# Strassen products on two halves of tokens, large down blocks and interleaved attentions in a one-core decoder step

## The chip, the cores and the metric

The kernel runs on one core of one Trainium2 chip. The metric is the device time of one execution in microseconds; less is better. The profile shows TensorE (PE, with its weight loads as PEld), VectorE (DVE), ScalarE (ACT), GpSimd (POOL), SyncE (SP) and the DMA engines. SBUF is the memory on the chip, PSUM holds what TensorE adds up.

## The reference

One layer of a hybrid decoder over 1104 tokens: 1040 of a prompt and 8 x 8 sample tokens, whose keys and values lie in a paged cache of 1024 positions for each of 8 sequences. All is float32, the model width 1024, the hidden width 2816.

```python
def layer(x, ...):
    x = x + 0.5 * rmsnorm(swiglu(rmsnorm(x, f1_pre), f1_wg, f1_wu, f1_wd), f1_post)
    m = mixer(rmsnorm(x, m_pre), w_in, ...)
    x = x + rmsnorm(m, m_post)
    x = x + 0.5 * rmsnorm(swiglu(rmsnorm(x, f2_pre), f2_wg, f2_wu, f2_wd), f2_post)

def swiglu(x, w_gate, w_up, w_down):
    return (jax.nn.silu(x @ w_gate) * (x @ w_up)) @ w_down

def mixer(h, ...):
    q, k, v, gate_b, gate_c, hc = jnp.split(h @ w_in, ...)      # 3072 columns
    o = rmsnorm(attend(q, k, v, lam), subln_g) * (1.0 - lambda_init)
    u_ext = concatenate([conv_prev, gate_c * hc], axis=1)
    y = sum(conv_w[j] * u_ext[:, j:j + t] for j in range(3))
    return concatenate([o, gate_b * y], axis=-1) @ w_out
```

`attend` is differential attention with 4 heads: for each head two softmax maps with 64 features of keys each, a weighted difference of the two, times 128 features of values. The prompt attends to itself causally, each sample sequence to its cached pages and its own new tokens.

## The kernel before, in words

Activations are kept with features on the partitions, in 8 chunks of 128, and tokens along the free dimension, in three groups `TG` of 376, 424 and 304. The array multiplies float32r, so every operand is kept as a high and a low half, and `three` (L187) makes a product of three matmuls, on lines 188, 189 and 190. `split_unit` (L170) loads 512 KB of weights, copies the high half (ACT, L177) and subtracts for the low one (POOL or DVE, L178).

A feed-forward (`ffn`, L343) goes through 11 blocks of two 128-wide hidden units. For each unit and group, `products` (L312) makes the gate and the up products, 24 matmuls into one PSUM bank; `gate` (L354) multiplies by 1 / rms, applies Silu, and multiplies again on POOL; `up_now` (L376) multiplies and splits the hidden values (DVE L381, ACT L382, DVE L383). `down` (L385) adds up two hidden units for each of 8 output chunks and 3 groups and adds the sum to `ys` in SBUF (DVE, L394). The hidden values never leave SBUF.

Between two phases stands `junction` (L258), for each token group: a mean over features by a matmul, a normalisation with the residual (DVE L279, POOL L280), high and low halves of the next phase's input (ACT, DVE L256), and sums of squares (L229). `meet` (L322) and the strings `FIRST`, `MEET1`, `MEET2`, `LAST` and `FINAL` (L70 to L76) write out by hand in which order the products of the last block, the junctions of the three groups and the first units of the next phase stand; `in_turn` ties a product behind the one before it on TensorE. Else a scheduler orders each engine's instructions.

The mixer makes q, k and v (12 units), stores high and low halves of q and k in DRAM, then makes the convolution's 12 units; the stages of the sample's attention stand between them (`turns`, L893): scores, weights, values and a gather for each of four pairs of sequences, with cache pages of 256 KB loaded ahead. Then comes the prompt's attention, 36 steps of head and query tile (`prompt_jobs`, L657): scores with high and low halves stacked on 128 rows (L675, L676), mask and maximum (DVE L684), exponents (ACT L696), difference of maps (POOL L700, DVE L701), transposes (L713), products with the values (L728). Between these steps stand the output projection's products for the convolution half (`conv_part`, L937). The rest of the output projection (`out_proj`, L1003) leads into the second feed-forward.

## Time and profile before

| | us |
|---|---|
| median of 3 runs | 2295.68 |
| lowest and highest of them | 2293.51, 2296.21 |
| span of the profiled execution | 2293.3 |
| PE busy in it | 2200.7 |
| DVE busy | 1064.4 |
| ACT busy | 601.9 |
| POOL busy | 656.0 |

The span is the time from the first to the last instruction of the one execution that was profiled; it lies 2.4 us under the median of the runs. A busy time is the sum over an engine's instructions with overlaps counted once. Matmuls are pipelined: the duration in a row is longer than the distance to the next start, so the pace of TensorE is read from starts.

### The profile page before, as it was taken

Reading aid. Unit: us, or ns where it says so; the run is one execution under the profiler, and the core shown is the slowest. Engines: PE = TensorE matmul, PEld = TensorE weight load, DVE = VectorE, ACT = ScalarE, POOL = GpSimd, SP = SyncE. Lnnn points to the kernel's source line nnn. Section 1 sums busy time; section 2 is a strip of 40 time slices with the busy share of each in tenths; the row PEclk is TensorE's granted clock in tenths of the full one; section 3 lists DMA queues with packets and bytes.
Section 4 is the critical chain, followed back from the end, with each engine's and each line's share of the span. In section 5 each row is a group of like instructions: output and inputs, shape, how many; then the busy total and the mean of one; then the engine's idle time right before and its main releaser. Section 6 shows DMA issues by size and latency. Waiting matters only on the chain.

```text
span 2293.3 us, 33252 instructions
## 1 busy us (share of the span) xinstructions
PE 2200.7 (96%) x13542; PEld 2126.0 (93%) x13542; DVE 1064.4 (46%) x1900; ACT 601.9 (26%) x1116; POOL 656.0 (29%) x487
## 2 busy tenths in 40 slices
PE   8999999999999899998998999899999999999995
PEld 7999999999999888997777899799999999999995
DVE  7333444343443587122226687943344343433347
ACT  6411111111111344211115565542111111111122
POOL 6222211222122355322223215641211222122215
PEclk9999999999999999998998999899999999999998
DMA  5101111111101142656677624421111111101113
GB/s 179 56 28 56 47 46 31 44 55 47 47 28 47 51 135 93 241 171 213 200 214 182 175 93 154 143 71 46 47 47 39 36 56 46 47 28 46 56 37 131
DMA packets 85387, 201.24 MB, mean 88 GB/s; under 512 B 18546, under 2 KB 38258, under 8 KB 82674
## 3 DMA queue, kind: packets, MB, share of 16 engines
q1 hardware_dynamic: 85234, 199.12, 27.3%
q8 instruction: 106, 1.74, 0.3%
q14 instruction: 47, 0.39, 0.1%
HBM read 161.80 MB, written 37.29 MB: 87 GB/s over the span
## 4 chain that ended last, share of the span: by engine, by line
PE 83%; DVE 8%; DMA 4%; ACT 2%; issue 1%; SPq 1%; POOL 1%; DVEq 0%; POOLq 0%; ACTq 0%
PE mm L188 18%; PE mm L189 18%; PE mm L190 18%; PE dn L188 8%; PE dn L189 8%; PE dn L190 8%; DVE y L279 3%; PE po L728 1%; DVE al L256 1%; DVE ss L229 1%; DMA raw<-oc_spill 1%; PE fl L713 1%; DMA raw<-in_w_out 1%; DMA qk<-qk_spill 1%; PE qk L675 1%
## 5 line engine op out<-in xcount | busy, mean ns | idle before, releaser
L189 PE MATMUL mm<-al,w 128*128 128x376 f32 (+2 forms) x2640 | 878.8, 333 | 16.1 <-DVE al L256 16.0
L188 PE MATMUL mm<-ah,w 128*128 128x376 f32 (+2 forms) x2640 | 880.4, 334 | 7.8 <-ACT w L177 5.4
L190 PE MATMUL mm<-ah,w 128*128 128x376 f32 (+2 forms) x2640 | 875.4, 332 | 0.5 <-DVE w L178 0.5
L189 PEld LDWEIGHTS mm<-al,w 128*128 128x128 f32 x2640 | 499.2, 189 | 29.2 <-DVE al L256 23.3
L188 PEld LDWEIGHTS mm<-ah,w 128*128 128x128 f32 x2640 | 499.1, 189 | 23.2 <-issue 8.7
L190 PEld LDWEIGHTS mm<-ah,w 128*128 128x128 f32 x2640 | 499.4, 189 | 6.7 <-DVE w L178 1.3
L178 POOL TENSOR_TENSOR w<-raw,w 128x1024 fp32r<-128x1024 f32 (+1 forms) x118 | 278.0, 2357 | 701.5 <-ACT w L177 696.9
L394 DVE TENSOR_TENSOR y<-y,dn 128x376 f32<-128x376 f32 (+2 forms) x480 | 255.3, 536 | 315.9 <-PE dn L190 315.5
L189 PE MATMUL dn<-w,w 128*128 128x376 f32 (+2 forms) x1056 | 350.1, 332 | 7.9 <-DVE w L383 7.9
L188 PE MATMUL dn<-w,w 128*128 128x376 f32 (+2 forms) x1056 | 348.6, 331 | 3.9 <-DVE y L394 3.9
L190 PE MATMUL dn<-w,w 128*128 128x376 f32 (+2 forms) x1056 | 349.7, 332 | 0.0
L177 ACT ACTIVATE w<-raw 128x1024 fp32r<-128x1024 f32 (+1 forms) x166 | 168.0, 1026 | 507.3 <-PE mm L189 224.7
L362 POOL TENSOR_TENSOR w<-w,R 128x376 f32<-128x376 f32 (+1 forms) x132 | 131.2, 996 | 582.4 <-ACT w L361 525.5
L361 ACT ACTIVATE w<-w 128x376 f32<-128x376 f32 (+1 forms) x132 | 66.0, 506 | 571.5 <-DVE w L357 571.4
L189 PEld LDWEIGHTS dn<-w,w 128*128 128x128 f32 x1056 | 199.4, 189 | 10.6 <-DVE w L383 8.6
L188 PEld LDWEIGHTS dn<-w,w 128*128 128x128 f32 x1056 | 199.1, 189 | 7.2 <-DVE y L394 5.1
L190 PEld LDWEIGHTS dn<-w,w 128*128 128x128 f32 x1056 | 199.4, 189 | 1.9
L357 DVE TENSOR_TENSOR w<-mm,R 128x376 f32<-128x376 f32 (+1 forms) x132 | 70.9, 540 | 260.1 <-PE mm L190 259.9
L383 DVE TENSOR_TENSOR w<-w,w 128x376 fp32r<-128x376 f32 (+1 forms) x132 | 148.7, 1129 | 66.8 <-ACT w L382 66.7
L381 DVE TENSOR_TENSOR w<-w,mm 128x376 f32<-128x376 f32 (+2 forms) x126 | 67.6, 536 | 225.1 <-PE mm L190 224.4
L382 ACT ACTIVATE w<-w 128x376 fp32r<-128x376 f32 (+2 forms) x132 | 66.5, 505 | 239.2 <-DVE w L381 239.2
L280 POOL TENSOR_TENSOR y<-y,xr 128x376 f32<-128x376 f32 (+2 forms) x66 | 81.8, 1269 | 47.4 <-DVE y L279 47.4
(153 smaller groups left out, 1875.2 us busy)
## 6 DMA issues: line engine op xcount, KB each, us to landing
raw<-in_w_gu SPq DMA_DIRECT2D x86, 512.0 KB, 3.7
raw<-in_w_dn SPq DMA_DIRECT2D x44, 512.0 KB, 3.6
kp<-in_cache_k SPq DMA_DIRECT2D x64, 256.0 KB, 4.5
vp<-in_cache_v SPq DMA_DIRECT2D x64, 256.0 KB, 4.7
raw<-in_w_in SPq DMA_DIRECT2D x24, 512.0 KB, 5.7
qk<-qk_spill SPq DMA_DIRECT2D x38, 260.0 KB, 6.2
qk_spill<-hl SPq DMA_DIRECT2D x8, 1040.0 KB, 4.1
w<-qk_spill SPq DMA_DIRECT2D x10, 260.0 KB, 7.9
```

What stands on the lines that cost most here:

```text
L177: nc.scalar.activation(hi[:, s], raw[:, s], AF.Copy)
L178: low_on.tensor_tensor(lo[:, s], raw[:, s], hi[:, s].bitcast(F32), op=ALU.subtract)
L188: nc.tensor.matmul(ps, lh, rh, start=first, stop=False)
L189: nc.tensor.matmul(ps, lh, rl, start=False, stop=False)
L190: last_pe[0] = nc.tensor.matmul(ps, ll, rh, start=False, stop=last).ins
L279: nc.vector.scalar_tensor_tensor(x, x, gains[:, g_post, c:c + 1], r, op0=ALU.mult, op1=ALU.mult)
L280: (nc.gpsimd if g_pre is not None or c < 6 else nc.vector).tensor_tensor(x, x, xs[c], op=ALU.add)
L357: nc.vector.tensor_tensor(g, pg, a[i][2], op=ALU.mult)
L362: nc.gpsimd.tensor_tensor(g, g, r, op=ALU.mult)
L381: nc.vector.tensor_tensor(v, v, pu, op=ALU.mult)
L383: nc.vector.tensor_tensor(hl, v, hh.bitcast(F32), op=ALU.subtract)
L394: nc.vector.tensor_tensor(ys[i][:, d, :], ys[i][:, d, :], ps, op=ALU.add)
```

## The change

The tokens are now two halves of 552, each of two quarters of 276 (`G`). The gate and the up product of a hidden unit, or two units of the input projection (`PAIRS`), are made for one half of tokens as a 2 x 2 block product by a Strassen scheme (Winograd's form): the input features in two halves, the two units, the two quarters of tokens. There are seven products instead of eight, each over 4 chunks of features and 276 tokens. Some are added up in a shared PSUM bank (`STEPS`), the others are combined on ACT and DVE (`Parts`, with `Hidden` for feed-forwards and `Unit2`, `Product`, `Gated` for the mixer). Both operands need sums: `weights_piece` adds quarters of the weights on DVE and splits each of the seven operands (ACT copy, DVE subtract, both 512 wide) into the only weight set there is, piece n behind product n of the unit before; `quarters_of` does the same once for each phase with the activations of a half.

```diff
+    STEPS = [("a", J_P1), ("b", J_Q5), ("a", J_Q6), ("c", J_P2), ("a", J_Q7), ("b", J_P3), ("a", J_Q4)]
+
+    def product(ps, p, j, first):
+        x14 = lay["x14"][p]
+        for k in range(4):
+            s = slice(k * P, (k + 1) * P)
+            three(ps, wset[:, j, 0, s], wset[:, j, 1, s], x14[:, 7 + j, k, :], x14[:, j, k, :],
+                  first and k == 0, k == 3, skip_group_check=True)
+
...
+        for i, (u, p) in enumerate(jobs):
+            change = i + 1 < len(jobs) and jobs[i + 1][0] != u
+            if p:
+                for _ in background:
+                    pass
+            use = uses(u, p)
+            banks = {}
+
+            def step(n, p=p, use=use, banks=banks):
+                tag, j = STEPS[n]
+                first = tag not in banks
+                if first:
+                    banks[tag] = bank("mm")[:, :G]
+                in_turn(product, banks[tag], p, j, first)
+                use(n, banks[tag])
+
+            def last(step=step, change=change):
+                step(6)
+                if change:
+                    weights_piece(6)
+                    order.pop(0)
+                    if order:
+                        weights_of(src(order[0]))
+
+            for n in range(6):
+                step(n)
+                if n == 0 and pending:
+                    pending()
+                if change:
+                    weights_piece(n)
+                for _ in range(BG):
+                    next(background, None)
+            pending = last
+        pending()
+        for _ in background:
+            pass
```

```diff
+    def weights_piece(n):
+
+        a11, a12, a22, a21 = [wraw[:, q, :] for q in range(4)]
+        a3 = WR[:, 2048:2560]
+        if n == 0:
+            dve.tensor_tensor(a3, a11, a21, op=ALU.add)
+        elif n == 1:
+            dve.tensor_tensor(a21, a21, a22, op=ALU.add)
+        elif n == 2:
+            dve.tensor_tensor(a11, a11, a21, op=ALU.add)
+        elif n == 5:
+            dve.tensor_tensor(a12, a12, a11, op=ALU.add)
+        halves(wset[:, n, 0, :], wset[:, n, 1, :], (a11, a21, a11, a12, a3, a12, a22)[n], dve)
...
+        def split(j, raw):
+            halves(x14[:, 7 + j, ks, :], x14[:, j, ks, :], raw, dve)
+
+        dve.tensor_tensor(t[0], b11, b12, op=ALU.subtract)
+        dve.scalar_tensor_tensor(t[1], t[0], -1.0, b22, op0=ALU.mult, op1=ALU.subtract)
+        split(0, b11)
+        split(1, t[0])
+        yield
+        dve.tensor_tensor(b12, b22, b12, op=ALU.subtract)
+        dve.scalar_tensor_tensor(t[2], t[1], -1.0, b21, op0=ALU.mult, op1=ALU.subtract)
+        split(2, t[1])
+        split(3, b21)
+        yield
+        split(4, b12)
+        split(5, b22)
+        split(6, t[2])
+        yield
```

The hidden values are written to DRAM and read back by `down`, which adds up 6, 6, 6 and 4 hidden units at a time (144 matmuls for 256 output columns and all tokens); the last 4 units are taken by halves of tokens, with the junction of half 0 between the sums of half 1, and the junction of half 1 as `background` of the next phase's `seven`. The first jobs of a phase are unit 0 and unit 1 on half 0, then unit 1 and unit 0 on half 1. The junction's residual add moves from POOL to DVE. The output projection goes through `down` too, in two blocks of four (convolution, then attention).

```diff
+                for c in PAIR_K:
+                    x = yv[p][:, c, :]
+                    dve.scalar_tensor_tensor(x, x, gains[:, g_post, c:c + 1], r, op0=ALU.mult, op1=ALU.mult)
+                    x3 = x.rearrange("p (g t) -> p g t", g=2)
+                    dve.tensor_tensor(x3, x3, xr[:, c // 4, c % 4], op=ALU.add)
+                    dma(dst[p][:, c, :], x)
```

The mixer writes q, k and v to DRAM; then the whole layout of SBUF is released and another one entered (`mix`). For each head q and k are loaded and split (two ACT copies and two DVE subtracts of 1040 columns). A map's scores are three matmuls on the 64 rows of that map. The stages of the sample's attention are spread over the 36 steps of the prompt's, and keys and values of the cache each have one ring of 8 pages.

```diff
+    def load_qk(h):
+        ql, kl, qh, kh = Q[h % 2]
+        for lo, hi, src in ((ql, qh, q_spill[h]), (kl, kh, k_spill[h])):
+            dma(f32(lo), src[:, :TP])
+            halves(hi, lo, f32(lo), dve)
...
+                k0, k1 = cuts[x], cuts[x + 1]
+                pw = [bank("qk")[:, :k1 - k0] for _ in range(2)]
+                ps = [w_[:rows] for w_ in pw]
+                for n, (a, b) in enumerate(((qh, kh), (qh, kl), (ql, kh))):
+                    for m in range(2):
+                        r = slice(m * DH, (m + 1) * DH)
+                        last_pe[0] = nc.tensor.matmul(pw[m], a[r, q0:q0 + P], b[r, k0:k1], start=n == 0, stop=n == 2,
+                                                      tile_position=(m * DH, 0)).ins
...
+    turns += [("v", last_pair, 0), ("g", last_pair - 1), ("v", last_pair, 1), ("g", last_pair)]
+    turns = [t for t in turns if t]
...
+    n_turns = len(turns)
...
+        while turns and (n_turns - len(turns)) * 32 < (step - 1) * n_turns:
+            stage(*turns.pop(0))
```

Three places of the built program, before and after. First DVE in the middle of a feed-forward: before, with the sums of a block of two (`L394`), the gate (`L357`), and the hidden splits (`L383`):

```order
L381 TENSOR_TENSOR w_2241<-w_2241,mm_2362 128x424
L383 TENSOR_TENSOR w_2358<-w_2241,w_2357 128x424
L381 TENSOR_TENSOR w_2241<-w_2241,mm_2390 128x304
L394 TENSOR_TENSOR y_268<-y_268,dn_2430 128x376
L383 TENSOR_TENSOR w_2358<-w_2241,w_2357 128x304
L394 TENSOR_TENSOR y_268<-y_268,dn_2438 128x376
L394 TENSOR_TENSOR y_269<-y_269,dn_2446 128x424
L394 TENSOR_TENSOR y_269<-y_269,dn_2454 128x424
L394 TENSOR_TENSOR y_270<-y_270,dn_2462 128x304
L394 TENSOR_TENSOR y_270<-y_270,dn_2470 128x304
L357 TENSOR_TENSOR w_2628<-mm_2629,R_258 128x376
```

After: weight sums (`L273` to `L279`), weight splits (`L169` into `W`), and the parts of the two products (`L350` to `L390`, `L367` times 1 / rms):

```order
L169 TENSOR_TENSOR W<-WR,W 128x512
L277 TENSOR_TENSOR WR<-WR 128x512
L390 SCALAR_TENSOR_TENSOR Y_79<-mm_1799,n_116_1812 128x276
L387 TENSOR_TENSOR Y_79<-u_1858,n_118_1844 128x276
L169 TENSOR_TENSOR W<-WR,W 128x512 x2
L350 TENSOR_TENSOR n_122_1920<-mm_1974,n_122_1920 128x276
L367 TENSOR_TENSOR n_122_1920<-n_122_1920,R_82 128x276
L169 TENSOR_TENSOR W<-WR,W 128x512
L353 SCALAR_TENSOR_TENSOR n_124_1952<-mm_1907,n_124_1952 128x276
L279 TENSOR_TENSOR WR<-WR 128x512
L169 TENSOR_TENSOR W<-WR,W 128x512
L356 TENSOR_TENSOR u_1969<-mm_1939,u_1969 128x276
```

The `L394` sums are gone from here, and each piece of the next weight set stands between the parts of the running unit.

Second DVE at the junction of the first feed-forward and the mixer. Before, group 2's normalisation and halves stand among the first q products (`L535`) of the groups done earlier:

```order
L219 SCALAR_TENSOR_TENSOR q_6926<-st_6924,q_6926 128x424
L220 SCALAR_TENSOR_TENSOR R_6923<-q_6926,R_6923 128x424
L535 TENSOR_TENSOR w_6788<-mm_7119,R_6923 128x424
L535 TENSOR_TENSOR w_6789<-mm_7145,R_6923 128x424
L535 TENSOR_TENSOR w_6790<-mm_7171,R_6923 128x424
L219 SCALAR_TENSOR_TENSOR q_6951<-st_6949,q_6951 128x304
L220 SCALAR_TENSOR_TENSOR r_6948<-q_6951,r_6948 128x304
L279 SCALAR_TENSOR_TENSOR y_270<-y_270,gains,r_6948 128x304 x8
L535 TENSOR_TENSOR w_6791<-mm_7197,R_6923 128x424
L256 SCALAR_TENSOR_TENSOR al_6959<-y_270,gains,ah_6958 128x304 x5
L229 TENSOR_TENSOR ss_6957<-ss_6957,sq_6976 128x304
L535 TENSOR_TENSOR w_6792<-mm_7223,R_6923 128x424
```

After, for the second half of tokens: quarter sums (`L236` to `L242`), splits of the seven operands (`L169` into `X_78`), sums of squares (`L210`), and the first weight split behind them (`L169` into `W`):

```order
L210 TENSOR_TENSOR ss_485_8312<-ss_485_8312,sq_8532 128x552
L236 TENSOR_TENSOR Y_79<-Y_80 128x552
L210 TENSOR_TENSOR ss_485_8312<-ss_485_8312,sq_8553 128x552
L169 TENSOR_TENSOR X_78<-Y_80,X_78 128x552
L237 SCALAR_TENSOR_TENSOR Y_79<-Y_79,Y_80 128x552
L241 TENSOR_TENSOR Y_80<-Y_80 128x2x276
L169 TENSOR_TENSOR X_78<-Y_79,X_78 128x552
L242 SCALAR_TENSOR_TENSOR Y_79<-Y_79,Y_80 128x552
L169 TENSOR_TENSOR X_78<-Y_80,X_78 128x552 x2
L169 TENSOR_TENSOR X_78<-Y_79,X_78 128x552
L169 TENSOR_TENSOR X_78<-Y_80,X_78 128x552
L169 TENSOR_TENSOR W<-WR,W 128x512
```

No row that reads a product of the mixer stands between them any more.

Third PE in the prompt's attention. Before, two matmuls a score map (`L675`, `L676`), transposes (`L713`), values (`L728`), and the products of `conv_part` (`L188` to `L190`):

```order
L188 MATMUL op_11320<-mc_11198,w_11264 128x424
L675 MATMUL qk_11696<-w_10468,w_10312 128x352
L676 MATMUL qk_11696<-w_10521,w_10312 128x352
L189 MATMUL op_11320<-mc_11198,w_11264 128x424
L190 MATMUL op_11320<-mc_11198,w_11265 128x424
L188 MATMUL op_11320<-mc_11198,w_11264 128x424
L189 MATMUL op_11320<-mc_11198,w_11264 128x424
L190 MATMUL op_11320<-mc_11198,w_11265 128x424
L675 MATMUL qk_11700<-w_10803,w_10646 128x336
L676 MATMUL qk_11700<-qk_11200,w_10646 128x336
L728 MATMUL po_11546<-at_11580,vs_11208 128x128 x6
L713 MATMUL fl_11656<-cst,p_11561 128x128 x4
```

After, three matmuls a map (`L780`) and the sample's scores (`L875`) from the key pages `kp`:

```order
L780 MATMUL qk_11819<-q_676_11215,q_675_11214 128x272
L780 MATMUL qk_11819<-q_674_11213,q_675_11214 128x272
L780 MATMUL qk_11819<-q_676_11215,q_673_11212 128x272
L780 MATMUL qk_11820<-q_676_11215,q_675_11214 128x272
L780 MATMUL qk_11820<-q_674_11213,q_675_11214 128x272
L780 MATMUL qk_11820<-q_676_11215,q_673_11212 128x272
L875 MATMUL sa_11657<-kp_11192,qs_11208 32x128 x4
L875 MATMUL sa_11657<-kp_11189,qs_11208 32x128 x4
L780 MATMUL qk_11879<-q_676_11215,q_675_11214 128x320
L780 MATMUL qk_11879<-q_674_11213,q_675_11214 128x320
L780 MATMUL qk_11879<-q_676_11215,q_673_11212 128x320
L875 MATMUL sa_11657<-kp_11193,qs_11208 32x128 x4
```

The stream products between the scores are gone, and matmuls that read cache pages stand in their place; the three matmuls of one map mostly stand together, then those of the other.

## Rows read from the trace of the kernel before

**Rows 1.** The page, parts 1 and 4: totals of each engine; the chain by engine.

```profile
PE 2200.7 (96%) x13542; PEld 2126.0 (93%) x13542; DVE 1064.4 (46%) x1900; ACT 601.9 (26%) x1116; POOL 656.0 (29%) x487
...
PE 83%; DVE 8%; DMA 4%; ACT 2%; issue 1%; SPq 1%; POOL 1%; DVEq 0%; POOLq 0%; ACTq 0%
```

**Rows 2.** Windows by stage: PE, PEld, DVE, ACT, POOL busy, clock, DMA share, GB/s.

```profile
0.00:12.00 12.00, 5.22 (x17) 4.13 (x17) 7.60 (x14) 6.83 (x15) 6.39 (x12) 1.00 0.79 245
12.00:780.00 768.00, 764.66 (x4527) 754.64 (x4526) 325.96 (x475) 166.09 (x271) 189.05 (x130) 1.00 0.16 51
780.00:900.00 120.00, 104.85 (x563) 96.50 (x562) 89.02 (x132) 57.24 (x101) 61.68 (x46) 0.93 0.31 100
...
1000.00:1210.00 210.00, 194.49 (x1653) 170.39 (x1652) 50.66 (x126) 22.90 (x33) 58.19 (x52) 0.95 0.67 199
1210.00:1390.00 180.00, 168.26 (x1086) 153.93 (x1085) 134.37 (x480) 112.98 (x302) 47.14 (x48) 0.96 0.57 160
1390.00:1500.00 110.00, 96.88 (x528) 90.73 (x526) 93.34 (x132) 56.59 (x114) 62.30 (x47) 0.94 0.41 137
1500.00:2263.00 763.00, 760.33 (x4533) 751.70 (x4534) 312.45 (x474) 152.64 (x243) 176.34 (x120) 1.00 0.15 49
2263.00:2293.00 30.00, 5.99 (x37) 4.93 (x35) 24.48 (x34) 7.09 (x14) 17.26 (x16) 0.66 0.26 100
```

**Rows 3.** The same windows, matmuls of line 189 alone: PE and PEld busy.

```profile
0.00:12.00 12.00, 2.70 (x6) 1.60 (x6) 1.00 0.79 245
...
780.00:900.00 120.00, 63.84 (x184) 35.87 (x183) 0.93 0.31 100
...
1000.00:1210.00 210.00, 91.22 (x273) 52.52 (x274) 0.95 0.67 199
1210.00:1390.00 180.00, 33.83 (x101) 19.10 (x102) 0.96 0.57 160
1390.00:1500.00 110.00, 55.49 (x157) 30.33 (x156) 0.94 0.41 137
...
2263.00:2293.00 30.00, 3.18 (x11) 1.88 (x10) 0.66 0.26 100
```

**Rows 4.** Windows, a coarser cut: the middle of the second feed-forward.

```profile
1600.00:2200.00 600.00, 600.00 (x3576) 593.81 (x3575) 238.09 (x366) 96.49 (x146) 125.09 (x82) 1.00 0.13 43
```

**Rows 5.** Timeline of PE: start, duration, line; 304 columns, later 272.

```profile
300.23 0.30 PE L188 MATMUL dn<-w,w 128*128 128x304 f32 x1
...
301.77 0.30 PE L190 MATMUL dn<-w,w 128*128 128x304 f32 x1
...
1349.33 0.29 PE L675 MATMUL qk<-qk,qk 128*128 128x272 f32 x1
...
1349.70 0.29 PE L676 MATMUL qk<-qk,qk 128*128 128x272 f32 x1
```

**Rows 6.** Lines by form, DVE: count, busy us, mean ns of one, idle before.

```profile
L394 DVE TENSOR_TENSOR y<-y,dn 128x424 f32<-128x424 f32 x160 | 94.8, 594 | 188.7 <-PE dn L190 188.6
L383 DVE TENSOR_TENSOR w<-w,w 128x304 fp32r<-128x304 f32 x44 | 93.5, 2124 | 18.9 <-ACT w L382 18.9
...
L394 DVE TENSOR_TENSOR y<-y,dn 128x304 f32<-128x304 f32 x160 | 75.2, 471 | 63.2 <-PE dn L190 63.2
...
L279 DVE SCALAR_TENSOR_TENSOR y<-y,gains,r 128x376 f32<-128x376 f32 x24 | 27.5, 1213 | 0.0
...
L383 DVE TENSOR_TENSOR w<-w,w 128x376 fp32r<-128x376 f32 x44 | 24.5, 557 | 27.1 <-ACT w L382 27.0
```

**Rows 7.** Waits of PE: matmul waiting, releaser, total us, times, longest.

```profile
PE mm L189 <- DVE al L256: 16.0, 15, 5.8
...
PE sa L823 <- DMA vp<-in_cache_v: 4.0, 3, 1.7
```

**Rows 8.** The page, part 6: DMA issues, count, KB each, us to landing.

```profile
raw<-in_w_gu SPq DMA_DIRECT2D x86, 512.0 KB, 3.7
...
kp<-in_cache_k SPq DMA_DIRECT2D x64, 256.0 KB, 4.5
```

1227 lines of the change are left out of this document (542 added, 685 removed).

## The prediction

> **What bounds the kernel now.** The page's totals come first: TensorE (PE) is busy for 96% of the span and stands in 83% of the chain that ended last [rows 1]. An average over stages hides where it is not, so the stages were read next, one window each [rows 2], with the matmuls of source line 189 counted in each window [rows 3]. Every float32 product is three matmuls, and line 189 is one of the three, so three times its count is the number of "stream" matmuls, those of the big projections. In the middle of the second feed-forward, 600 us hold 3576 matmuls without a gap, 167.8 ns each at full granted clock [rows 4]. Subtracting 3 x count x 0.1678 us from each window leaves what the stream did not fill: 12 - 3 = 9 us at the start, 120 - 92.6 = 27.4 at the first junction, 210 - 137.4 = 72.6 where the sample's attention runs beside the convolutions, 180 - 50.8 = 129.2 in the prompt's attention, 110 - 79 = 31 at the second junction, 30 - 5.5 = 24.5 at the tail. That is about 294 us; the feed-forward windows lose some 10 more, and 11808 stream matmuls x 0.1678 = 1981 us are the rest of 2293. So two things can be gained: fewer columns through PE, and less of those 294 us.
>
> **Fewer columns.** Before, 3936 matmuls of each of three widths (376, 424, 304). After, gate, up and input units cost 7 products of 4 chunks x 3 matmuls for two 128-column units and one half of tokens: 22 pairs x 2 halves x 84 = 3696 in each feed-forward and 12 x 2 x 84 = 2016 in the mixer; the down products are 2112 in each feed-forward and the output projection 768, no longer Strassen. All together 14400 matmuls of 276 columns, 22% more instructions with 9% fewer columns. The price of one is the start-to-start interval, which I read at the two nearest widths [rows 5]: 304 columns 1.54 us / 11 = 140.0 ns, 272 columns 0.37 us / 3 = 123.3 ns. A straight line between them gives 125.4 ns at 276, scaling the 304-column row by columns gives 127.1. I take 126.4: 14400 x 0.1264 = **1820 us**, 161 less, with 1806 and 1830 as ends.
>
> **What is added on VectorE (DVE), steady state.** PSUM adds cost 471 ns at 304 and 594 at 424 columns [rows 6], so 1.025 ns a column: 442 ns at 276, 684 at 512, 725 at 552. A gate/up unit of the order of instructions (both halves of tokens) has 11 DVE operations of 512 and 14 of 276 columns: 7.5 + 6.2 = 13.7 us. PE needs 168 x 126.4 = 21.2 us for it. The DVE work lies beside PE and costs nothing; with that cover gone it would be 13.7 us for each of 56 units. The single weight set is rewritten piece by piece behind the product that read it, and a piece is wanted again 7 products (10.6 us) later, while its split takes 0.7 us; a raw load is twice the 512 KB that land in 3.7 us [rows 8] and is asked for a product into the job before the one that needs it. Only where two neighbouring jobs both change the unit (the fourth job of a phase) is that late, by some us. The down items are 144 matmuls (18.2 us) against 8 adds, DVE is idle there. The hidden units now go through DRAM; the first loads of a down stage stand behind the last unit, so I put 5 us for each of two hand-overs, 10.
>
> **The edges become DVE-bound.** A Strassen phase may not start its products on half 1 before every quarter sum of that half is made and split. At the start DVE has, ahead of the last of them, 61 operations of 276, 36 of 552 and 25 of 512 columns: 27.0 + 26.1 + 17.1 = 70 us, after some 6 us of loading (512 KB in 3.7 us [rows 8]); PE has only the two jobs on half 0 to fill that, 21.2 us. Lost: **55** (before: 9). At the first junction DVE has 75 of 552, 73 of 276 and 12 of 512 columns: 54.4 + 32.3 + 8.2 = 95 us, and 4 for the two means; PE has the last down sums of half 1 (192 x 0.1264 = 24.3 us) and the two jobs on half 0 (21.2). Lost: 99 - 45.5 = **53** (before 27, with DVE busy for only 89 of 120 us [rows 2]). The second junction has the same list, **53** (before 31). The same wait exists now in small: PE on DVE's activation halves, 16.0 us [rows 7]. Lower end for each junction 27, what it costs now; upper end 60. The residual adds moved from GpSimd to DVE remove the slow case of the row "L279", 1213 ns at 376 columns beside GpSimd, where a clean one by the line above is 545; that is in my prices already. Tail: 16 operations of 552 columns, 12 us, means and the last stores, **20** (now 24.5).
>
> **The attentions.** The two stages cost 72.6 + 129.2 = 202 us beside the stream, which covered the sample's page loads (137 us of stream) and filled gaps in the prompt's part (51 us). After, neither cover is there; the two attentions cover each other. PE's own work: the prompt window had PE busy 168.3, less 50.8 of stream is 117.5 [rows 2, 3]; scores go from two matmuls a map to three at 64 rows. One pass over all keys is 38016 columns x 0.453 ns (272 in 123.3) = 17.2 us, so 117.5 + 17.2 = 135. The sample adds at most 194.5 - 137.4 = 57; part of that is time at a lower granted clock (mean 0.95), so I put 40. Sum 175. DVE: 134 now, plus 8 splits of 1040 columns at 1.2 (10 us) and the sample's 12: 156. Neither engine runs at 100% through a chain of score, maximum, exponent, difference, transpose; 180 us held 168 of PE. I take **200**, with 175 (PE only) and 235 (202 + 17 + 16, covering each other hardly at all) as ends. Entering, the constants, queries and keys of head 0 are loaded behind the mixer's last instruction: two loads and 2.5 us of splits, 15; leaving, the same for the output projection, 13: **28** together. The mean granted clock is below 1.00 in the windows in which PE idles (0.93 at the first junction, 0.66 in the tail [rows 2]); longer idle stretches cost more of it: **8**.
>
> A rule speaks for less here. The score matmuls of the two maps sit in different row halves of the array, and the order sets mostly three of one map, then three of the other, which is why I charge six slots. The Trainium skill (TensorE: Matmul & The Clock Gate, Part 3: Packing small matmuls) says that matmuls at different tile positions run at the same time; were that so for every pair, the sum would be some 26 us lower, 2219. No row of the kernel before shows two row halves in use.
>
> **Sum.** 1820 + 55 + 53 + 53 + 20 + 10 + 28 + 200 + 8 = 2247 against 2293 in this profiled execution. The span of the profile is 2.4 us under the median of the runs, which I neglect beside my bounds: I predict **2245 us**, 2.2% less than the median of 2295.68.
>
> **Rivals.** *Overlap is better than I charge* (0.24). Attention at its lower end, 175, and each junction halfway to what it costs now, 40: 2247 - 25 - 26 - start at 45 (-10) = 2186. For it: DVE's junction list has independent operations and the scheduler puts the next unit's weights between. Against it: the list is 95 us long by rows of single operations.
>
> *Pages not hidden* (0.13), on the other side. The sample's caches come as 16 batches of 8 cache pages, 2.1 MB each, in one ring of 8 for keys and one for values, so a batch is asked for only when the one before it was multiplied. At the 199 GB/s of the sample's window [rows 2] a batch takes 10.5 us; a page lands 4.5 us after issue [rows 8]. A turn lasts 200 / 26 = 7.7 us, and there are two to three turns between a batch and its use, so 15 us against 10.5: hidden, if SyncE's queue is free. But page loads stand in that queue behind stores that wait for DVE, and PE executes the sample's matmuls in order, ahead of the prompt's. Now it already waits for value pages three times, 4.0 us [rows 7]. Each exposed microsecond of a batch costs 16 us: it decides from 2293 - 2247 = 46, / 16 = 2.9 us a batch; at 5 us a batch 2327.
>
> *GpSimd slows DVE* (0.05). The same subtraction takes 557 ns at 376 columns and 2124 ns at 304, where GpSimd is at work [rows 6], 1.65 us more than 0.47. In a unit DVE has 7.5 us to spare. Four GpSimd products a unit, each hitting one DVE operation, take 6.6: still covered. From 5 hits a unit the time is lost; 6 hits are 13.7 + 9.9 = 23.6, 2.4 us over, x 56 units = 134: 2381. The Trainium skill (GPSIMD Engine Reference, 1. Specifications) names the cause: its SBUF interfaces are shared with VectorE, against instructions with two SBUF inputs, which here are the weight splits. This trace agrees, by those 2124 ns.
>
> *The change doesn't do what it says* (0.02). If a narrower matmul started no sooner than the 304-column ones, 14400 x 0.140 = 2016 and the total 2443. The 272-column row at 123 ns speaks against it.
>
> **How the numbers follow.** My forecast 0.53, reaching from 2200 to 2285 by the ends above; better overlap 0.24; pages 0.13; GpSimd 0.05; no narrower interval 0.02; 0.03 for an outcome within 0.2%, some 5 us, about what a measurement of this kernel can tell from no change. Faster 0.53 + 0.24 = 0.77, same 0.03, slower 0.20. The range takes in the forecast, the rival of better overlap to some 20 us below its figure, and pages at 5 us a batch: 2165 to 2330. Outside are GpSimd and the unchanged interval (0.07), and some 0.1 of the tails.
>
> **What would show it.** Stream: windows in mid feed-forward at PE 100% and 126 ns a matmul; at over 130 the first term is wrong. Edges: PE idle for about 50 us at the start and at each junction, released by DVE's splits (line 169), DVE near 100% in them; PE waiting under 35 there means that I overcharged. Steady units: DVE some 65% busy; a PE wait for a weight split in mid-phase means contention. Attentions: a block of about 200 us plus 28 around it; waits of the sample's matmuls for pages summing to over 46 us would be the slower rival. The whole is wrong if the time is over 2330 or under 2165.

## The result and the profile after

The change makes the kernel slower: **2344.34 us** (median of 4 runs, 2341.6 to 2346.7) against 2294.86 (2293.51 to 2296.21), ratio 1.0219 [1.0204, 1.0233]. The forecast of 2245 had the wrong sign, and the range ended at 2330.

The page after, parts 1, 4 and 6 (as [rows 1, 8]):

```profile
span 2344.9 us, 40781 instructions
...
PE 2123.6 (91%) x16266; PEld 2036.9 (87%) x16266; DVE 1373.3 (59%) x2698; ACT 908.3 (39%) x1830; POOL 325.5 (14%) x360
...
PE 78%; DVE 11%; DMA 5%; ACT 3%; issue 2%; SPq 1%; POOL 0%; DVEq 0%; ACTq 0%
...
WR<-in_w_in SPq DMA_DIRECT2D x13, 1024.0 KB, 5.4
```

PE is busy 77 us less than before, as it was meant to be; yet the span is 52 us longer. The windows by stage say where (columns as in [rows 2]; the last but one is mid feed-forward, as [rows 4]):

```profile
0.00:91.00 91.00, 53.32 (x333) 50.02 (x334) 73.72 (x152) 71.18 (x135) 6.48 (x12) 0.91 0.45 156
790.00:900.00 110.00, 65.39 (x433) 60.61 (x432) 94.78 (x177) 66.73 (x132) 12.07 (x12) 0.77 0.31 110
900.00:1136.00 236.00, 223.50 (x1701) 222.58 (x1701) 128.40 (x216) 68.05 (x138) 58.79 (x67) 0.96 0.31 90
1136.00:1150.00 14.00, 0.30 (x3) 0.08 (x1) 3.87 (x4) 3.32 (x4) 1.18 (x3) 0.64 0.71 241
1150.00:1200.00 50.00, 37.20 (x251) 27.43 (x252) 20.24 (x83) 13.08 (x38) 6.12 (x22) 0.50 0.68 222
1200.00:1350.00 150.00, 146.06 (x1321) 101.36 (x1320) 101.71 (x383) 76.02 (x199) 18.80 (x25) 0.99 0.57 187
1350.00:1372.00 22.00, 21.73 (x73) 14.53 (x74) 11.41 (x45) 8.98 (x23) 2.43 (x3) 0.50 0.33 102
1372.00:1403.40 31.40, 22.95 (x143) 16.00 (x142) 16.47 (x44) 14.78 (x35) 2.16 (x2) 0.93 0.16 48
1504.00:1610.00 106.00, 55.52 (x359) 51.06 (x358) 87.50 (x171) 77.06 (x142) 6.13 (x7) 0.74 0.23 81
1700.00:2300.00 600.00, 595.58 (x4654) 594.51 (x4653) 308.66 (x523) 192.92 (x372) 87.46 (x84) 1.00 0.26 87
2300.00:2345.00 45.00, 18.18 (x130) 16.92 (x128) 33.16 (x56) 7.38 (x14) 0.00 (x0) 0.73 0.43 151
```

The same windows, matmuls of line 162 alone (one of the three of each product, as line 189 was in [rows 3]):

```profile
0.00:91.00 91.00, 35.15 (x109) 23.03 (x109) 0.91 0.45 156
790.00:900.00 110.00, 43.01 (x141) 27.69 (x140) 0.77 0.31 110
900.00:1136.00 236.00, 164.93 (x555) 107.12 (x555) 0.96 0.31 90
1504.00:1610.00 106.00, 36.02 (x116) 22.91 (x115) 0.74 0.23 81
2300.00:2345.00 45.00, 11.91 (x42) 7.73 (x41) 0.73 0.43 151
```

A stream matmul's start-to-start distance is 127.7 ns (mean of those that waited for nothing; the mid feed-forward row agrees: 595.6 us / 4654 = 128.0, other matmuls among them). Taking stream x 0.1277 from each window, as the prediction did with 0.1678, gives what the stream did not fill. In the column before, the mixer's row comes from one more window of line 189 (prediction's price):

```profile
900.00:1000.00 100.00, 63.42 (x192) 35.94 (x191) 1.00 0.56 205
```

| us | before | forecast | after |
|---|---|---|---|
| stream | 1981 | 1820 | 1839 |
| start | 9 | 55 | 49.5 |
| first junction | 27.4 | 53 | 56.5 |
| mixer, up to the attentions | 3 | 0 | 23.5 |
| attentions, entry and exit with them | 202 | 236 | 267 |
| second junction | 31 | 53 | 62 |
| tail | 24.5 | 20 | 29 |
| what is left, hand-overs in it | 15 | 10 | 18 |

The stream gave back 142 us, and the other rows took 193. Waits of PE (columns as in [rows 7]):

```profile
PE mm L162 <- ACT X L168: 100.6, 13, 25.3
PE mm L163 <- DVE X L169: 15.4, 14, 3.4
...
PE mm L162 <- DVE n L353: 14.0, 5, 4.3
PE qk L780 <- ACT q L168: 13.9, 1, 13.9
...
PE sa L875 <- POOL qs L746: 7.5, 4, 6.8
PE sa L875 <- DMA kp<-in_cache_k: 4.2, 2, 3.0
```

The edges' waits (ACT's copies of the activations, line 168) stand first; the pages that were a rival of the forecast, last.

### The profile page after: what moved, and what is told of

Read it like the earlier page. It is cut to its first block, busy times and chain, and to the rows that moved or that the text cites. A ratio compares the mean times of both kernels' runs of the same rounds, so it can differ in the third digit from the quotient of the medians.

```text
span 2344.9 us, 40781 instructions
## 1 busy us (share of the span) xinstructions
PE 2123.6 (91%) x16266; PEld 2036.9 (87%) x16266; DVE 1373.3 (59%) x2698; ACT 908.3 (39%) x1830; POOL 325.5 (14%) x360
## 4 chain that ended last, share of the span: by engine, by line
PE 78%; DVE 11%; DMA 5%; ACT 3%; issue 2%; SPq 1%; POOL 0%; DVEq 0%; ACTq 0%
PE mm L162 23%; PE mm L163 23%; PE mm L164 23%; DVE X L169 2%; PE qk L780 2%; PE po L833 2%; DMA WR<-in_w_in 2%; DVE W L169 1%; DVE Y L469 1%; PE fl L818 1%; PE sa L910 1%; PE sa L875 1%; DVE ss L210 1%; DVE Y L467 1%; DMA WR<-in_w_gu 1%
## 5 line engine op out<-in xcount | busy, mean ns | idle before, releaser
L162 PE MATMUL mm<-X,W 128*128 128x276 f32 x4224 | 1240.8, 294 | 141.1 <-ACT X L168 100.6
L163 PE MATMUL mm<-X,W 128*128 128x276 f32 x4224 | 1238.7, 293 | 13.4 <-DVE X L169 12.8
L164 PE MATMUL mm<-X,W 128*128 128x276 f32 x4224 | 1234.2, 292 | 5.2 <-DVE W L169 5.2
L162 PEld LDWEIGHTS mm<-X,W 128*128 128x128 f32 x4224 | 803.6, 190 | 148.5 <-ACT X L168 104.2
L163 PEld LDWEIGHTS mm<-X,W 128*128 128x128 f32 x4224 | 804.3, 190 | 17.9 <-DVE X L169 16.3
L164 PEld LDWEIGHTS mm<-X,W 128*128 128x128 f32 x4224 | 805.0, 191 | 7.2 <-DVE W L169 6.7
L168 ACT ACTIVATE W<-WR 128x512 fp32r<-128x512 f32 (+1 forms) x437 | 292.7, 674 | 614.5 <-PE mm L163 526.4
L169 DVE TENSOR_TENSOR W<-WR,W 128x512 fp32r<-128x512 f32 (+1 forms) x437 | 333.9, 766 | 194.0 <-ACT W L168 164.4
L367 POOL TENSOR_TENSOR n<-n,R 128x276 f32<-128x276 f32 x88 | 70.2, 798 | 675.1 <-ACT n L378 675.1
L350 DVE TENSOR_TENSOR n<-mm,n 128x276 f32<-128x276 f32 x112 | 49.8, 445 | 155.2 <-PE mm L164 155.1
L347 ACT ACTIVATE n<-mm 128x276 f32<-128x276 f32 x224 | 87.7, 392 | 117.0 <-PE mm L164 105.0
L367 POOL TENSOR_TENSOR u<-u,R 128x276 f32<-128x276 f32 x88 | 77.9, 885 | 292.2 <-ACT u L378 292.2
L169 POOL TENSOR_TENSOR X<-X 128x552 fp32r<-128x552 f32 x46 | 75.8, 1658 | 303.0 <-ACT X L168 275.7
L169 DVE TENSOR_TENSOR X<-X 128x552 fp32r<-128x552 f32 x58 | 65.2, 1147 | 79.5 <-ACT X L168 79.5
L163 PE MATMUL mm<-X,X 128*128 128x276 f32 x288 | 83.8, 291 | 2.6 <-DVE X L169 2.6
L163 PE MATMUL mm<-X 128*128 128x276 f32 x288 | 84.2, 292 | 0.0
L780 PE MATMUL qk<-q,q 64*128 64x400 f32 (+10 forms) x360 | 69.5, 392 | 16.1 <-ACT q L168 13.9
L162 PE MATMUL mm<-X,X 128*128 128x276 f32 x288 | 83.5, 290 | 0.0
L164 PE MATMUL mm<-X,X 128*128 128x276 f32 x288 | 83.4, 290 | 0.0
```

Of the source, the lines that this page charges most:

```text
L162: nc.tensor.matmul(ps, lh, rh, start=first, stop=False, **kw)
L163: nc.tensor.matmul(ps, lh, rl, start=False, stop=False, **kw)
L164: last_pe[0] = nc.tensor.matmul(ps, ll, rh, start=False, stop=last, **kw).ins
L168: act.activation(hi, raw, AF.Copy)
L169: on.tensor_tensor(lo, raw, f32(hi), op=ALU.subtract)
L347: act.activation(t, ps, AF.Copy)
```

## The experiments

Times are medians; the kernel before lay between 2294.8 and 2297.4 in all calls. "Minus n" is against the change's 2344.3. Each diff shows the main lines of its edit.

### The scheme itself

**Strassen undone** (`e4_direct`): eight direct products of 4 chunks; halves, attentions and all else stay.

```diff
-    STEPS = [("a", J_P1), ("b", J_Q5), ("a", J_Q6), ("c", J_P2), ("a", J_Q7), ("b", J_P3), ("a", J_Q4)]
+    STEPS = [("a", 0, 0), ("a", 1, 2), ("b", 2, 1), ("b", 3, 3), ("c", 0, 1), ("c", 1, 3), ("d", 2, 0), ("d", 3, 2)]
```

> The Strassen scheme alone is undone: eight direct products of quarters, no sums of quarters, four weight splits in place of seven; tokens, blocks, junctions and attentions stay. Theory: 1344 stream matmuls more at 127.7 ns are +172 us; DVE has 12 + 10 us less of quarter sums and splits and 5 us less of weight splits ahead of the products at each of three edges, about -25 each; time 2344 + 172 - 75 = 2441. Rival (the scheme saves nothing, since sums and splits bound the steady part): 2344 or less.

2419.71 us, 1.0544 [1.0522, 1.0565]. The scheme saves 75 us net. Eight products for seven are a seventh more of the 9408 gate, up and input matmuls, 1344 x 0.1277 = 172 us; 97 of them are given back. In this kernel's windows, read as above, the start costs 30 us, the first junction 37, the second 45.6 and the mixer 2.6, against 49.5, 56.5, 62 and 23.5: 76 of the 97. The other 21 weren't followed. Its longest edge wait shows the same:

```profile
PE mm L162 <- ACT X L168: 67.6, 13, 17.1
```

So the loss against before isn't Strassen's: without it this rewrite stands 125 us over the kernel before.

### The attentions

**The sample's attention left out** (`e3_nosample`; its output is zero, its loads and matmuls are gone):

```diff
-        while turns and (n_turns - len(turns)) * 32 < (step - 1) * n_turns:
-            stage(*turns.pop(0))
+    gp.memset(o_t, 0.0)
```

> The sample's attention is left out altogether (its loads, scores, weights, values and gathers; zeros go on). Theory (TensorE-bound block): its 69 us between starts and a part of the low clock go, the block falls from 267 to about 185 us, the time to about 2262. Rival (the sample is hidden in gaps of the prompt's chain): the block falls by under 20 us.

2289.57 us, 0.9968 [0.9941, 0.9996]. The block from the mixer's last to the output projection's first matmul fell from 267 to 218 us: 49 us, of the 57 that the forecast had as the most that the sample adds (55 between the medians; this kernel's runs lie between 2272 and 2300 us, the profiled one at 2298). Summed by line from each PE start to the next, with time at 0.50 counted as half, the sample's matmuls take 57 us in the change and the prompt's 140; here the prompt's take 140 again. So the sample isn't covered by the prompt's attention, since both want PE. The block falls by less than that because the prompt alone, though it keeps PE busy, runs at half clock for longer: 99 us of its work, against 62 us of both in the change (windows of this run):

```profile
1150.00:1200.00 50.00, 45.84 (x190) 34.46 (x191) 34.20 (x127) 25.46 (x65) 7.64 (x10) 0.57 0.20 71
1250.00:1300.00 50.00, 48.93 (x187) 35.91 (x187) 26.70 (x106) 19.80 (x54) 5.43 (x7) 0.53 0.06 20
```

**Score matmuls of the two row halves in turn** (`e1_pairs`): each is issued after the one before it, so that the maps alternate.

```diff
-                        last_pe[0] = nc.tensor.matmul(pw[m], a[r, q0:q0 + P], b[r, k0:k1], start=n == 0, stop=n == 2,
+                        with tc.issue_after(pair[0]) if pair[0] is not None else nullcontext():
+                            pair[0] = nc.tensor.matmul(pw[m], a[r, q0:q0 + P], b[r, k0:k1], start=n == 0, stop=n == 2,
```

> The score matmuls of the two maps alternate on TensorE, one on each row half of the array. Theory (the block of both attentions is bound by TensorE, and three matmuls of one map in a row take a slot each): two row halves run at the same time, the 69 us between starts behind the score matmuls fall to about 40, the block of 267 us to about 240, the time from 2344 to about 2317. Rival (the block is bound by the chain maximum, exponent, difference, transpose on the other engines): under 5 us.

2333.55 us, 1.018 [1.0147, 1.0213]: minus 11. Summed from each PE start to the next, waits included, scores fall from 69 to 58 us, not to half. The trace says why. The two halves of a pair do start together, 3 to 4 ns apart at full clock, but in the change 75 of the 168 pairs of over 16 columns already started less than 40 ns apart; here it is 147. And a pair can take longer than one matmul: at 400 columns the next pair follows after 284 or after 178 ns, where two matmuls of one half stand 182 ns apart. Why it is sometimes 284 stays open. Without waits, and with time at 0.50 counted as half, the scores fall from 53 to 46 us. The clock comes back earlier too, and work at 0.50 falls from 62 to 31 us, but that isn't shown to be the edit's: with scores and sample as in the change it is 33 us in the profile of `e8_entry`, 34 in `e6_sspe` and 76 in `e11_adds_pool`. So some 7 of the 11 us are the pairs' own (windows of this run):

```profile
1150.00:1200.00 50.00, 32.58 (x257) 21.90 (x257) 21.14 (x88) 14.76 (x41) 6.11 (x22) 0.64 0.65 222
1200.00:1390.00 190.00, 173.94 (x1528) 118.07 (x1528) 128.66 (x465) 98.76 (x254) 22.38 (x30) 0.98 0.51 170
```

**Both** (`e10_pairs_nosample`, sample left out):

> Alternating row halves, with the sample's attention left out (zeros go on), against the kernel that leaves it out with the order as it was: there the prompt's attention alone takes 197 us at a mean clock of about 0.75. If TensorE at a low clock sets that time, some 40 us go (17 us a pass at full clock, three passes fewer, at twice the price for half of the time); if the chain over DVE and ACT sets it, under 15 us.

2271.47 us, 0.9885 [0.9864, 0.9907]. The prompt's block alone goes from 218 to 193; with the sample beside it the pairs' block is 253, so the sample adds 60. Neither theory's number was met, but the sample is uncovered either way.

**Warming at the entry** (`e2_warm`): 90 unused whole-array matmuls while head 0 is loaded.

```diff
+    warm = bank("qk")[:, :G]
+    for _ in range(90):
+        last_pe[0] = nc.tensor.matmul(warm, W[:, :P], W[:, 1024:1024 + G], start=True, stop=True).ins
```

> 90 matmuls of 276 columns on old weights are added at the entry of the attentions, where TensorE stands idle for 14 us. Theory (the granted clock of 0.50 from 1150 to 1200 us comes of that idle stretch and doubles the price of the matmuls there): clock near 1.00 behind the entry, about 20 us less, 2324. Rival (the sparse, narrow matmuls themselves do not hold the clock up): the clock falls to 0.50 again within a few us, and the time is the same within 5 us.

2340.39 us, 1.0202 [1.0178, 1.0227]: minus 4 at most. Full clock at the entry, and lost again behind it:

```profile
1135.00:1148.00 13.00, 11.62 (x94) 11.15 (x92) 3.16 (x6) 2.60 (x4) 1.10 (x2) 1.00 0.66 240
1148.00:1200.00 52.00, 37.10 (x280) 24.58 (x281) 24.33 (x92) 15.84 (x42) 6.12 (x22) 0.61 0.65 218
```

**Whole-array filler between the scores** (`e13_fill`): 240 unused matmuls, to price the clock.

```diff
+                for _ in range(4):
+                    last_pe[0] = nc.tensor.matmul(pw[0], W[:, 6144:6272], W[:, 6272:6272 + k1 - k0], start=True, stop=True).ins
```

> Four matmuls over the whole array on old weights are put ahead of each of 60 score pieces, as wide as it, into its bank (overwritten by the scores): 240 x 317 columns, 35 us of work that nobody needs. If low granted clock is what the attentions pay for, it is at 1.00 for longer and the time rises by far less than 35 us, or falls; if TensorE's work alone counts, 2344 + 35 = 2379.

2370.41 us, 1.0324 [1.0307, 1.034]. The clock holds from 1200 us on:

```profile
1140.00:1200.00 60.00, 43.83 (x299) 31.99 (x299) 24.42 (x92) 17.57 (x43) 6.39 (x23) 0.63 0.69 233
1200.00:1400.00 200.00, 198.96 (x1611) 139.59 (x1609) 118.98 (x430) 87.64 (x224) 22.93 (x29) 1.00 0.46 152
```

The filler takes 52 us from start to start, the block grows by 22 (267 to 289), so the rest fell by 30: some 19 are shorter matmuls, as work at 0.50 fell from 62 to 30 us, and some 10 are idle time in which filler now stands. This doesn't show that filler holds the clock, as `e8_entry` and `e6_sspe` have 33 and 34 us at 0.50 without it. What the low clock costs is read from the rows of after: 37.2 + 21.7 us of busy PE stand in its two windows at 0.50, and half of that is 29.5. As a mend the filler loses.

**The sample started three steps later, its inputs ahead of its pages** (`e7_late`):

```diff
+    sample_inputs()
     load_keys(0, 0)
     load_values(0, 0)
-    sample_inputs()
...
-        while turns and (n_turns - len(turns)) * 32 < (step - 1) * n_turns:
+        while turns and (n_turns - len(turns)) * 29 < (step - 4) * n_turns:
```

> The sample's attention begins three prompt steps later and its queries, keys and values of the new tokens are loaded ahead of the cache pages. Theory (TensorE's in-order waits for the sample's first inputs, 7.5 + 4.2 us, and the low clock that follows them are a fault of the start): 10 to 25 us less, about 2326. Rival (the start is latency of the prompt's chain; the waits only move): under 5 us.

2346.86 us, 1.0227 [1.0207, 1.0247]: nothing. Moving sample work along the block doesn't change how much of it PE has.

**Head 0's constants, queries and keys loaded ahead** (`e8_entry`, into memory of the operands of half 0, asked for on GpSimd's queue):

```diff
-    dma(cst, ins["consts"])
+    def early(dst, src):
+        got = gp.dma_start(dst, src)
+        last_dma[0] = got.ins
...
-    load_qk(0)
-    load_v(0)
+    load_qk(0, early)
+    load_v(0, early)
```

> What the prompt's attention needs first (constants, q, k and v of head 0) is placed where half 0's operands lay and asked for on GpSimd's queue, so that it can come during the mixer's last job. Theory (14 us of entry are transfers and splits behind the last store of the mixer): 8 to 12 us less, about 2334. Rival (the place is not free earlier, or the queue is blocked): no change.

2336.07 us, 1.0167 [1.0146, 1.0188]. The wait that it was aimed at stayed, so its 8 us aren't from there. The block is 7 us shorter (260), with 33 us of work at 0.50 in place of 62; whether the edit has a part in that is open:

```profile
PE qk L785 <- ACT q L168: 15.7, 1, 15.7
```

### The mixer's gaps

In after, DVE at 1024 us:

```profile
1023.94 0.69 DVE L273 TENSOR_TENSOR WR<-WR 128x512 f32<-128x512 f32 x1 [6.55 <-DMA WR<-in_w_in]
1024.55 0.44 DVE L353 SCALAR_TENSOR_TENSOR n<-mm,n 128x276 f32<-128x276 f32 x1
```

The sum of weights waits 6.55 us for its raw weights, and the PSUM read that PE waits for (line 353) stands behind it on DVE. The DMA view of 1005 to 1030 us names what the weights stand behind:

```profile
WR<-in_w_in SPq DMA_DIRECT2D x1, 1024.0 KB, 10.5
...
out_conv_s<-Y SPq DMA_DIRECT2D x1, 8.0 KB, 8.8
```

10.5 us against the page's median of 5.4, behind a store of the convolution state: 8 KB in runs of 8 bytes. **The state through a contiguous tile** (`e5_contig`), so that a run has 64 bytes; the load of the two rows goes through such a tile as well:

```diff
-        dma(outs["conv_s"][j], us[:, :, 8:10])
+        gp.tensor_copy(st_out[j % 2], us[:, :, 8:10])
+        dma(outs["conv_s"][j], st_out[j % 2])
```

> The convolution's two rows of state go in and out through a tile in which they lie together (two small copies on GpSimd more), so a store has 128 runs of 64 bytes in place of 1024 of 8. Theory (the three waits of some 4.5 us in the mixer come of the raw weights standing in the DMA queues behind those stores: 10.5 us to landing in place of 5.4): the load lands in 5 to 6 us, the waits of TensorE for line 353 go, and with them the low clock there; 12 to 20 us less, about 2328. Rival (the waits come of DVE's 1040-wide convolution steps): under 4 us.

2324.12 us, 1.0114 [1.0093, 1.0135]: minus 20, and the first score matmul starts at 1131.5 us, against 1150.2 in the change. The store lands in 2.5 us (DMA view of 1000 to 1030 us):

```profile
out_conv_s<-Y SPq DMA_DIRECT2D x1, 8.0 KB, 2.5
```

And PE is busy throughout the window of 1000 to 1056 us, where the change's own had 47.5 at a clock of 0.90:

```profile
1000.00:1056.00 56.00, 56.00 (x438) 55.78 (x437) 40.85 (x67) 17.98 (x36) 20.34 (x27) 1.00 0.19 55
```

### The edges

The forecast had them bound by DVE's list. In the two stretches of the first junction in which PE stands idle most, DVE is nearly full (columns as in [rows 2]):

```profile
800.00:820.00 20.00, 5.55 (x17) 3.84 (x18) 19.56 (x48) 17.31 (x38) 0.00 (x0) 0.55 0.29 99
840.00:880.00 40.00, 12.73 (x71) 11.13 (x70) 36.87 (x59) 23.52 (x42) 1.84 (x2) 0.62 0.22 82
```

The rows of line 210 in after (DVE adds a chunk's squares, which ACT made in line 209, in the only tile `sq`) show turns beside that:

```profile
its engine sat idle before it (us, times) until:
  ACT sq L209: 17.2, 24
who waited for it (us, times):
  ACT sq L209: 34.2, 26
```

ACT may write the tile only when DVE has read it, DVE waits for ACT to write it. The tail, on DVE:

```profile
2318.62 0.73 DVE L210 TENSOR_TENSOR R<-R,sq 128x552 f32<-128x552 f32 x1 [0.73 <-ACT sq L209]
2320.08 0.73 DVE L210 TENSOR_TENSOR R<-R,sq 128x552 f32<-128x552 f32 x1 [0.73 <-ACT sq L209]
```

1.46 us a chunk, where DVE alone needs 0.73. Four runs take the tile and the adds apart (the sums of squares of the next phase's input, 42 of the 84 adds, move to PE as 192 matmuls; DVE keeps the others):

| us | adds on DVE | on PE |
|---|---|---|
| one tile of 552 | 2344.3 (the change) | 2346.3 `e9_sspe1` |
| two tiles of 276 | 2330.9 `e12_sqhalf` | 2316.1 `e14_sspehalf` |
| two tiles of 552 | no room in memory | 2291.6 `e6_sspe` |

The edit of `e6_sspe`; `e9_sspe1` is this with one tile, `e14_sspehalf` with two half tiles:

```diff
-        ss2 = temp("ss2", HT)
+        sums_of = [bank("st")[:, :G] for _ in range(2)]
...
-            sq_add(ss2, x, n == 0)
+            sq = temp("sq", HT, 2)
+            act.activation(sq, x, AF.Square)
+            for half in range(2):
+                nc.tensor.matmul(sums_of[half], onesD, sq[:, half * G:half * G + G], start=n == 0, stop=n == C - 1,
```

> The sums of squares of the next phase's input are added up by TensorE over the 8 chunks in PSUM, in place of 14 adds of 552 columns on DVE at each of three edges, and the tile of squares has two buffers. Theory (edges are bound by DVE's list): 14 x 0.73 = 10 us less at each, and some of the alternation of ACT and DVE on the one buffer goes: 30 to 40 us, about 2308. Rival (ACT, which makes every high half and every square there, is as late as DVE): under 10 us.

2291.55 us, 1.0 [0.9977, 1.0024]: minus 53, more than expected. PE's waits in it:

```profile
PE st L258 <- ACT sq L256: 23.7, 15, 5.3
...
PE mm L162 <- ACT X L168: 11.8, 6, 6.6
```

Line 168's 100.6 us are 11.8. With one tile, the first of PE's waits is:

```profile
PE st L258 <- ACT sq L256: 65.1, 32, 17.4
```

> As the sums of squares on TensorE, but with the one tile of squares that the changed kernel has. If the gain of 53 us came of DVE's list being shorter by 14 adds an edge, this stays within 10 us of it (2290 to 2302); if it came of ACT and DVE no longer taking turns on one tile, most of it goes (2320 or more).

2346.34 us, 1.0204 [1.0186, 1.0223]: with one tile, taking the adds off DVE gains nothing; the wait only changes its name, as ACT may now write the tile only when PE has read it. DVE is no longer full in such stretches of the first junction (this run):

```profile
800.00:820.00 20.00, 14.05 (x55) 11.22 (x56) 15.67 (x37) 16.48 (x36) 0.00 (x0) 0.66 0.00 1
850.00:870.00 20.00, 15.39 (x59) 11.01 (x60) 13.45 (x21) 17.44 (x29) 0.00 (x0) 0.80 0.19 69
```

The adds on DVE, two half tiles:

```diff
-            sq = temp("sq", HT)
-            act.activation(sq, src, AF.Square)
-            dve.tensor_tensor(ss, ss, sq, op=ALU.add)
+            for g in range(2):
+                part = slice(g * G, g * G + G)
+                sq = temp("sq", G, 2)
+                act.activation(sq, src[:, part], AF.Square)
+                dve.tensor_tensor(ss[:, part], ss[:, part], sq, op=ALU.add)
```

> The adds of squares stay on DVE, but the one tile of 552 squares is made two of 276, taken in turn; each add is two of 276 columns, so DVE has 0.15 us more for each of 28 at a junction. If the edges were long because ACT and DVE take turns on one tile, most of the 53 us come back without TensorE's sums: 2295 to 2315. If it was DVE's list, the time rises: 2350.

2330.86 us, 1.0141 [1.0122, 1.016]: minus 13, between the two theories.

> The next layer's sum of squares is made on TensorE as in the run with two whole tiles of squares, but with two tiles of half the width (the fourth corner: one tile with VectorE's adds is the change itself, 2344; one tile with TensorE 2346; two half tiles with VectorE's adds 2331). If both must go (a second tile so that ScalarE may run ahead, and VectorE's adds off its list), two half tiles do what two whole ones did: 2290 to 2300. If whole tiles are needed, because half tiles double ScalarE's instructions and leave it just as short a lead, it stays at 2325 to 2335.

2316.07 us, 1.01 [1.0077, 1.0124]: minus 28, again between them. So neither half of the edit sets the edge alone: with two half tiles the adds are worth 15 us, with one they are worth nothing, and with PE adding, whole tiles gain 25 on half ones. DVE's list and the tile's turns form one chain. The attentions' block, which these edits don't touch, takes 259 to 275 us in their profiles (267 in the change), so differences of some 8 us in the table say nothing.

**The residual adds of the junctions on GpSimd again** (`e11_adds_pool`):

```diff
-                    dve.tensor_tensor(x3, x3, xr[:, c // 4, c % 4], op=ALU.add)
+                    (dve if g_pre is None else gp).tensor_tensor(x3, x3, xr[:, c // 4, c % 4], op=ALU.add)
```

> The residual adds of both junctions are back on GpSimd, as before the change. If DVE's list alone sets the junctions, 16 adds of 0.73 us go from it at each of two: up to 23 us less. If GpSimd's slower add (1.3 us at 376 columns in the kernel before) stands in the chain of the chunk and slows DVE beside it, no gain or a loss of up to 20 us.

2362.38 us, 1.028 [1.026, 1.03]: 18 slower. This doesn't tell whether DVE's list is the bound, because the list didn't get shorter. The normalisation of line 467 takes longer beside GpSimd's adds, which take 1842 ns each (the change's row, then this run's, columns as in [rows 6]):

```profile
L467 DVE SCALAR_TENSOR_TENSOR Y<-Y,gains,R 128x552 f32<-128x552 f32 x48 | 34.4, 789 | 0.2
L467 DVE SCALAR_TENSOR_TENSOR Y<-Y,gains,R 128x552 f32<-128x552 f32 x48 | 60.6, 1330 | 0.2
```

That is 48 x 541 ns = 26 us more on DVE, against 32 adds of 0.73 us, 23 us, that left it.

### Together

**Contiguous state, squares on PE, early loads and alternating row halves** (`b1_all`):

> Four edits together: alternating row halves (11 us alone), the state in one piece (20), squares added up on TensorE with two buffers (53), the early load at the entry (8). Theory (they lie in different stages and add up): 92 us less than 2344, about 2252, faster than the kernel before by 2%. Rival (they share time, the early entry and the pairs above all, or one gives back what another won): 2275 or more.

**2265.8 us, 0.9871 [0.9851, 0.9891]**: faster than both kernels. The four gained 11 + 20 + 53 + 8 = 92 singly and 78 together. PE is busy for 95% of this span (2140.0 us).

The entry to the attentions is as it was (its waits of PE):

```profile
PE qk L795 <- ACT q L168: 14.2, 1, 14.2
```

Two runs held the output projection's first weights back to the fifth step of the attentions. `b2_all` did so without the early loads, and with the constants of `mixer_constants` later:

```diff
+            with tc.issue_after(hold[0]) if hold[0] is not None else nullcontext():
+                dma(raw, wsrc)
...
+        if step == 4:
+            hold[0] = last_dma[0]
```

> The state in one piece, squares on TensorE, alternating row halves, and at the entry of the attentions the output projection's weights and the lambda constants later, so that ACT's copies of q and k stand first in its order. If the 14 us of entry are that order, 6 to 10 us come off: about 2258. If they are the transfers of q and k themselves, 2266 as the other combination.

2275.06 us, 0.9896 [0.9878, 0.9914], over both figures and 9 over `b1_all`, which has the early loads. And `b3_all` with them:

> The best combination so far (contiguous convolution state, squares on TensorE in two tiles, constants and head 0's queries and keys loaded ahead, alternate row halves; 2265.8) with the first loads of the output projection's weights held back to the fifth step of the attention, so that VectorE's splits of them do not stand ahead of the first scores. If they hold the entry, 2254 to 2261; if head 0's own loads and copies hold it, as the rival says, within 4 us of 2266.

2266.39 us, 0.9871 [0.985, 0.9892], from 2257 to 2271. The wait at the entry fell by 3 us, to 11.2, and the time did not move beyond its scatter.

What holds the remaining 11 us of the entry stays open.

## Why the prediction was wrong

**Stream.** Right in kind, 19 us short. The price was read between two rows [rows 5] as 126.4, with 125.4 and 127.1 as ends; it is 127.7, over the upper one and nearest to the 304-column row scaled by columns. The 272-column row that pulled it down was a mean over three matmuls. The rival *no narrower interval* fell with it.

**The attentions are the step that failed.** Forecast 200 + 28 + 8 = 236, measured 267. The windows divide it: 14 us of entry, 25.5 of idle PE inside the block and at its exit (12.8 + 3.9 + 0.3 + 8.5), 29.5 lost to the clock, and the rest, 198.5, is PE's work at full clock. Two terms were mis-sized. PE's work was put at 135 + 40 = 175, 23.5 too low, most of it in the sample: "part of that is time at a lower granted clock (mean 0.95), so I put 40" took 17 off the 57 us which, by line, its matmuls do fill at full clock (the prompt's fill 140). The clock was put at 8, for idle stretches, 21.5 too low: PE was granted 0.50 for 22 us in which it was busy for 21.7. (In the profiles of the other runs with these scores and the sample it cost 16 to 38, over 8 in each.) Idle PE, with entry and exit, was put too high, 25 + 15 + 13 against 14 + 25.5. So covering was not the fault: the forecast added the two attentions on PE, and its waits were enough. What it didn't see is that without the stream between the scores, where the clock was 0.95 and 0.96 [rows 2], a busy PE can be granted 0.50. That the stream had held the clock up is argued and not shown: `e13_fill` put whole-array matmuls back and had no less time at 0.50 than runs without them. The stage rose by 65 us and the forecast allowed 34.

**The mixer** was put at 0 and cost 23.5, where it had been 3: 12.1 in three of the five waits for line 353, up to 4.3 each, and a lower granted clock behind them (0.90 from 1000 to 1056 us). A weight load is "twice the 512 KB that land in 3.7 us" was the price, and what stands ahead of it in the queue wasn't read. `e5_contig` shows this cause, 20 us of it.

**The edges** came out near the forecast, 49.5 + 56.5 + 62 + 29 = 197 for 181, by a mechanism that was half of the truth. DVE is 86% busy over the first junction (94.8 of 110), and 98% and 92% in the stretches in which PE stands idle, so its list did bound them, as forecast. But it was not the only bound: `e9_sspe1` takes 42 adds off the list and gains nothing, since the one tile then holds up ACT and PE. And PE is released by ACT's copies (line 168, 100.6 us) far more than by DVE's splits (line 169, 15.4), which the forecast had named.

**Hand-overs.** The row of 18 is what all other rows leave. PE's waits around the two hand-overs (500 to 560 and 2030 to 2070 us) sum to 4.0 and 3.7 us, under the 5 put for each; where the rest lies wasn't followed.

**Rivals.** *Better overlap* fell: the attentions (175) and the junctions (40) came nowhere near its figures. *Pages not hidden*: the waits for key pages are 4.2 us, far from the 46 at which it decides. *GpSimd slows DVE* fell: in mid feed-forward PE is busy for 595.6 of 600 us, though DVE's weight sums of line 277 take 1137 ns there beside GpSimd and the equal ones of line 275 only 692. The slower outcome came by none of them; it is the sum of three terms that were 74 us too low together (19 + 23.5 + 31), and of the edges and the last row of the table, 16 and 8 over. The Trainium skill (TensorE: Matmul & The Clock Gate, Part 3: Packing small matmuls) says that matmuls at different tile positions run at the same time. The trace of `e1_pairs` agrees as to the starts, 3 to 4 ns apart. The 26 us that the forecast saw in it did not come: 75 of 168 pairs started so in the change already, where the forecast charged six slots throughout, and a pair could take longer than one matmul; alternating took 11 us off, some 7 of them in the scores themselves.

## What to carry to other kernels

Two phases that both want the same engine don't cover each other: price them by the sum on that engine, and take nothing off a measured busy time for a low clock unless a row shows how much. A busy engine is no proof of a full clock: look at the granted clock of each stretch, in several profiles. A saving in products is paid for at every edge where operands are made: count there not only operations an engine, but scratch tiles that two engines pass to and fro. And read what stands in the queue ahead of each load that must be in time, by its runs and not by its bytes.
